# A hybrid decoder block: one spatial-gate product moves to head 6, one to the front of head 0, and the last row-sum turn goes behind an output product

## The chip, the cores and the metric

The kernel runs on one core of one Trainium2 chip. The metric is the device time of one execution in microseconds (us), lower is better. The core has TensorE (PE, with its weight loads shown as PEld), VectorE (DVE), ScalarE (ACT), GpSimd (POOL) and SyncE (SP, which issues nearly all DMAs here).

## The reference

The block takes x of 1024 tokens x 1024 channels in float32. Cut to what matters here:

```python
proj = rmsnorm(x, g1) @ w_in                 # q, k, v: 512 columns each; u, vg: 512 each; 8 forget gates
log_f = log_sigmoid(forget + b_forget)
att = forgetting_attention(q, k, v, log_f)   # 8 heads of 64; softmax(q k / 8 + c_i - c_j, causal) v
u, vg = split(gelu(uv))                      # 8 groups of 64 columns
sg = u * (tril(w_spatial) @ rmsnorm(vg) + b) # mixing inside chunks of 128 tokens
h = x + concat(att, sg) @ w_out              # 512 attention rows and 512 gate rows of w_out
h = h + conv_ffn(rmsnorm(h, g2), ...)        # up to 2 x 2816, causal conv of 3, silu gate, down
return rmsnorm(h, g_final)
```

## The kernel before

The work goes through stages: the projections, the spatial gate, attention, the output projection with the second norm, the up-projection with the convolution, and the down-projection. Matmul operands are split into a high part (rounded to fp32r) and the low rest, and each product is three matmuls: high x high, high x low, low x high. Except where the code fixes an order, the instructions of ScalarE, VectorE, GpSimd and SyncE are put in order at build time by a planner, which takes the earlier in the program among those whose inputs it expects to be ready. On TensorE the helper `seq` chains all instructions of the attention stage, so there the program's order holds.

**Attention.** The eight heads are cut into steps, `STEPS` (L1190), five for each head; step n is step `s = n % 5` of head `h = n // 5`, and holds two groups of attention blocks (the fifth holds one). The loop from L1226 does, in step n:

- `turn_p` (L1080) for the groups of step n+1: transposes of exponentials into a PSUM bank, a ScalarE cast to the high half (L1094) and a VectorE subtraction to the low half (L1095), both into a tile `pt`, of which there are three;
- `values` (L1100) for the groups of step n, on those halves (L1109), and where a half head is complete the evacuation to `attF` (L1117, L1118);
- for each group, the logits of one query block of the next head: four or fewer matmuls (L1021, L1022) into one of two buffers, and a VectorE pass (L1038) that adds the mask and takes the row minimum; the exponentials (L1062) come on ScalarE one step later;
- `fill` (L1194), which takes the next product of the spatial gate if `FILLS` (L22) names this step;
- copies of exponentials by DMA (`copy_p`, L1048), which make later transposes cheaper.

**Spatial-gate products.** `sg_out` (L1127) is a generator of 16 products, eight token blocks for each half of the output columns. Each is 12 matmuls (L1143 to L1145) of the transposed gate result `sgT` (four tiles, tag G) with split weights `whs` (four tiles, tag whl), a residual block loaded ahead (L1125), a VectorE add (L1147) and a store to `hpd` (L1148). At the seventh product the weights of the second half are loaded (`sg_load`); after the eighth, the list `SPLIT` has four splits, which the loop makes at L1295 to L1300, high half on ScalarE, low half on GpSimd. Three products stand before the loop (keys with head -1), the others in heads 0 to 5.

**Output projection, attention part.** `wo_load` (L1164) is called in step 35. It loads the four row blocks of `w_out` for attention and splits each on GpSimd (L1176, L1177), the first two into whl tiles and the other two into G tiles, four buffers of each tag. `pair_half` (L978) multiplies a pair of heads by its reciprocal row sums and splits it, on GpSimd (L984 to L986) for the first three pairs and on VectorE and ScalarE (L988 to L992) for the last; the third pair's result is a G tile too. `wmm` (L1180) makes output products (L1185); `EARLY` (L1188) puts those of the second and third weight block into steps 36 and 37.

**Row sums.** `row_tail` (L967) transposes the reciprocal row sums of a head (L972), copies them (L973), sends them to memory (L974, ScalarE's queue) and loads them back spread over 64 partitions (L975, SyncE's queue).

Of the kernel before, what the change touches and what calls it, by code (L numbers as in the profile page):

```python
# [18 lines left out]
NFF = 22  # L19
WARM = 8  # L20

FILLS = {(-1, j): 1 for j in (6, 4, 2)} | {(h, s): 1 for h in range(6) for s in ((0, 2, 4) if h == 0 else (2, 4))}  # L22
FCFG = ("b", 4, 4)


# [38 lines left out]
def after(tc, later, earlier):  # L64
    tc.add_manual_dep(later.ins, earlier.ins.name, mybir.DependencyInfo(
        mybir.DependencyClass.NoSync, mybir.DependencyReason.DATA), reason="order")
# [8 lines left out]
def block_kernel(ctx: ExitStack, tc: tile.TileContext, xT, xtok, wuv, wuh, wv0, wva, wvk, wvl, wqk, cpk, bfv,  # L75
# [10 lines left out]
    drm = ctx.enter_context(tc.tile_pool(name="drm", bufs=1, space=bass.MemoryType.DRAM))  # L86
    FILL = FILLS
    FTAG, FB, BB = FCFG
# [13 lines left out]
    def sb(tag, shape, dt=F32):  # L102
        return (base if tag == "x1" else raws if tag == "raw" else late if tag in LATE else early).tile(shape, dt, tag=tag, bufs=BUFS[tag], name=nm(tag))
# [10 lines left out]
    def f32(ap):  # L114
        return ap.bitcast(F32)
# [15 lines left out]
    for _ in range(WARM):  # L131
# [11 lines left out]
                       fill=MASK, base=0, channel_multiplier=1)  # L143
# [57 lines left out]
    def xs(n, hl, k):  # L201
        return XS[n][k // 2][hl][:, k % 2, :]
# [7 lines left out]
    def xr(n, k):  # L210
        return RAW[n][k // 2][:, k % 2, :]
# [89 lines left out]
    for o in (slice(0, 256), slice(256, 512)):  # L301
        h, l, src = xs("B11", 0, 0)[:, o], xs("B11", 1, 0)[:, o], xr("x11", 0)[:, o]
# [662 lines left out]
    exs, turns, due_copies, copied = [], {}, [], []  # L965
# [82 lines left out]
    def copy_p(h, i, ld=None):  # L1048

        w1, w2 = (2 * i + 1) * P, (2 * i + 2) * P  # L1050
        c = COLS[i] * P
        w1, w2 = w1 - c, w2 - c
        tp = sb(CTAG[i], [P, w1 + w2])
        turns[h, i] = (tp[:, 0:w1], tp[:, w1:w1 + w2])
        for jj in (1, 0):
            copied[:] = [sp.dma_start(out=turns[h, i][jj], in_=places[h, i][jj][:, c:])]
            if ld:
                after(tc, copied[0], ld)
# [62 lines left out]
    def residuals():  # L1121
        for hf in range(2):
            for tt in range(8):
                hs = sb("raw", [P, 512])
                yield hs, sp.dma_start(out=hs, in_=xtok[tt * P:(tt + 1) * P, hf * 512:hf * 512 + 512])  # L1125

    def sg_out(whs):  # L1127
        ready, source = [], residuals()
        for hf in range(2):
            o = slice(hf * 512, hf * 512 + 512)  # L1130
            for tt in range(8):
                ts_ = slice(tt * P, (tt + 1) * P)
                while len(ready) < (2 if due_copies else 1):
                    ready.append(next(source))
                while due_copies:
                    copy_p(*due_copies.pop(0), ready[-1][1])
                if hf == 0 and tt == 6:
                    nxt = sg_load(1, copied[0])
                hs = ready.pop(0)[0]
                ps = fbank()  # L1140
                for k in range(4):
                    w = whs[k]
                    seq(pe.matmul(ps, sgT[k][:, 0, ts_], w[:, 0, :], start=(k == 0), stop=False))  # L1143
                    seq(pe.matmul(ps, sgT[k][:, 0, ts_], w[:, 1, :], start=False, stop=False))  # L1144
                    seq(pe.matmul(ps, sgT[k][:, 1, ts_], w[:, 0, :], start=False, stop=(k == 3)))  # L1145
                def evac(ps=ps, hs=hs, tt=tt, o=o):
                    dve.tensor_tensor(out=hs, in0=ps, in1=hs, op=ALU.add)  # L1147
                    sp.dma_start(out=hpd[tt, :, o], in_=hs)  # L1148

                if dve.on:  # L1150
                    EVAC.append(evac)
                else:
                    evac()
                if hf == 0 and tt == 7:
                    whs = [None] * 4
                    SPLIT[:] = [(whs, k, nxt[k]) for k in range(4)]
                yield

    EVAC, SPLIT = [], []
# [20 lines left out]
    def wmm(tt, hf, ps, ks_):  # L1180
        ts_ = slice(tt * P, (tt + 1) * P)
        for k in ks_:
            w = wo[k][hf]
            for n, (a, b) in enumerate(((0, 0), (0, 1), (1, 0))):
                seq(pe.matmul(ps, attT[k][:, a, ts_], w[:, b, :], start=(k == 0 and n == 0), stop=(k == 3 and n == 2)))  # L1185

    banks8 = {}
    EARLY = {36: (1,), 37: (2,)}  # L1188
# [5 lines left out]
    def fill(key):  # L1194
        for _ in range(FILL.get(key, 0)):
            next(filler, None)
# [29 lines left out]
    for n, step in enumerate(STEPS):  # L1226
        h, s = n // 5, n % 5
        if s == 0 and h < 6:
            head_loads(h + 2)
        if h == 7 and s == 0:  # L1230
            for _ in filler:
                pass
            wo_load((0, 1))
            wo_load((2, 3))
        if h in (2, 4, 6) and s == 4:
            for o in (slice(0, 512), slice(512, 1024)):
                pair_half(h // 2 - 1, o)
        now, turned = turned, []
        last, due = due, []
        if n == 35:  # L1240
            psl.release()
            psl = tc.alloc_tile_pool(name="psc", bufs=4, space=bass.MemoryType.PSUM, reuse_waits="tile")
            banks8[0, 0] = lbank()
            wmm(0, 0, banks8[0, 0], (0,))
        for g in STEPS[n + 1] if n + 1 < len(STEPS) else []:
            if n == 36 and turned:
                for e in held + [mrow]:
                    after(tc, logits_exp(*e), casts[-1])
            turned.append(turn_p(g))
            if n == 36 and len(turned) == 2:  # L1250
                after(tc, casts[-1], exs[-1])
        if n == 34:
            mrow = (7, 0, logits_min(7, 0, mrow))
        if n == 33:

            held, last = last, []
        if n == 34:
            last, held = held[:1], held[1:] + last
        if n == 35:
            last, held = held[:1], held[1:]  # L1260
        if s == 1 and h % 2 == 0:
            attF[h // 2] = sb("H", [P, 2, 1024])
        if s == (1 if h < 7 else 2):
            recips[h] = dve.reciprocal(rows[h], rows[h])
        out_copy = None
        if n == 37:
            row_tail(7)
        if n in EARLY:
            wmm(0, 0, banks8[0, 0], EARLY[n])
        if n == 39:  # L1270
            banks8[4, 0] = lbank()
            wmm(4, 0, banks8[4, 0], (0,))
        for c, (g, pt, js) in enumerate(zip(step, now, NEXT[s])):
            out_copy = values(g, pt) or out_copy
            last_copy = out_copy
            if h < 7:
                for j in js:
                    if n == 33 and j == 0:
                        mrow = logits_mm(7, 0, place())
                        continue  # L1280
                    due.append((h + 1, j, logits_min(h + 1, j, logits_mm(h + 1, j, place()))))
            if s == 1 and h < 7 and c == 0:
                row_tail(h)

        for e in last:
            x = logits_exp(*e)
            after(tc, x, casts[-1] if n == 34 else out_copy or casts[-1])
        if s == 2 and h < 7:
            due_copies.extend(((h + 1, 3), (h + 1, 2)) if h < 6 else ((7, 3),))
        fill((h, s))  # L1290
        if s > 2 and h < 6:
            due_copies.append((h + 1, 4 - s))
        while due_copies:
            copy_p(*due_copies.pop(0))
        for _ in range(min(len(SPLIT), 1 if n == 9 else 2)):  # L1295
            ws_, k, wr = SPLIT.pop(0)
            wt = sb("whl", [P, 2, 512], F32R)
            ws_[k] = wt
            after(tc, act.copy(wt[:, 0], wr), out_copy or casts[-1])
            pool.tensor_tensor(out=wt[:, 1], in0=wr, in1=f32(wt[:, 0]), op=ALU.subtract)  # L1300
        if n == 2:
            vh = sb("A", [P, 2, 4, 256])
            sp.dma_start(out=vh, in_=vu.rearrange("h p m c -> p h m c"))
        if n in UPPER:
            tt = UPPER.index(n)
            v = V[tt // 2][:, tt % 2, 4:8]
            src = vh[:, tt // 4, tt % 4, :].rearrange("p (h d) -> p h d", h=4)
            after(tc, act.activation(src, src, AF.Copy, scale=rstd1[:, tt:tt + 1]), exs[-1])
            pool.tensor_copy(v[:, :, 0, :], src)
            pool.tensor_tensor(out=v[:, :, 1, :], in0=src, in1=f32(v[:, :, 0, :]), op=ALU.subtract)  # L1310
# [631 lines left out]
```

## Time and profile before

| what | us |
|---|---|
| median of 3 runs (1041.4 to 1042.5) | 1042.24 |
| the profiled execution, its time | 1042.4 |
| its span, first to last instruction | 1040.4 |
| TensorE busy | 1031.9 (99%) |
| VectorE busy | 890.5 (86%) |
| ScalarE busy | 563.7 (54%) |
| GpSimd busy | 242.2 (23%) |

In the profiled execution the projections and the gate end at about 207 us, the products before the loop at 223, the loop at 357, the output projection at 404, the up-projection at 825. Head 0 with its three products takes from 225.1 to 245.3; heads 1 to 5, with two each, some 17.7 each; from 333.8 the logits of head 7 have no product beside them.

Timeline rows give start, length, engine, line, operation and tiles, and in brackets the idle time of the engine before it with what ended it. Consecutive instructions of one kind are merged (x12), and a matmul's length overlaps with the next one's.

### The profile page before, as it was taken

The numbers are of one execution on the slowest core, as the hardware profiler recorded it, in microseconds if no ns is written. First come the engines' busy times: TensorE is split into PE (matmuls) and PEld (weight loads), VectorE is DVE, ScalarE is ACT, GpSimd is POOL, SyncE is SP. The second block draws the span as 40 slices with busy tenths as digits, with TensorE's granted clock in tenths as the row PEclk, the third lists the DMA queues.
The fourth block names the chain that finished last, engine by engine and source line by source line (L and its number), as shares of the span: only waits on it lengthen the run. The fifth ranks groups of instructions, "written<-read, shape, count | busy, mean of one in ns | idle before, by whom it ended". The sixth has DMA issues, their size and how long they took to land.

```text
span 1040.4 us, 14435 instructions
## 1 busy us (share of the span) xinstructions
PE 1031.9 (99%) x4998; PEld 865.6 (83%) x4998; DVE 890.5 (86%) x1294; ACT 563.7 (54%) x1004; POOL 242.2 (23%) x195
## 2 busy tenths in 40 slices
PE   9999999999999999999999999999999999999997
PEld 6988888988888888888888888888888888888886
DVE  6899887888888888998999998998997866997774
ACT  6777533457876757654444443444544554444654
POOL 0000242512733640433334323333331000000000
PEclk9999999999999999999999999999999999999999
DMA  9622558897978652231354432432322998333432
GB/s 336 221 97 83 163 150 247 232 252 224 275 249 258 231 165 99 82 122 62 136 178 139 132 115 72 132 101 86 116 82 93 324 332 294 110 92 101 149 117 99
DMA packets 73708, 170.25 MB, mean 164 GB/s; under 512 B 8718, under 2 KB 12934, under 8 KB 73636
## 3 DMA queue, kind: packets, MB, share of 16 engines
q1 hardware_dynamic: 73364, 169.30, 50.8%
q8 instruction: 39, 0.64, 0.2%
q14 instruction: 33, 0.27, 0.1%
q10 hardware_dynamic: 272, 0.04, 0.0%
HBM read 112.53 MB, written 45.05 MB: 151 GB/s over the span
## 4 chain that ended last, share of the span: by engine, by line
PE 94%; DVE 2%; ACT 2%; DMA 1%; issue 1%; SPq 0%; ACTq 0%; DVEq 0%
PE pb L1488 23%; PE pk L1488 17%; PE pb L1752 11%; PE pk L1752 9%; PE ps L286 4%; PE pk L1185 4%; PE pb L1109 3%; PE pb L286 3%; PE qc L525 2%; PE qd L525 2%; PE qa L525 2%; PE ps L876 2%; PE pl L1021 1%; PE pl L1022 1%; PE pf L1143 1%; PE pf L1144 1%
## 5 line engine op out<-in xcount | busy, mean ns | idle before, releaser
L1488 PE MATMUL pb<-xT,whb 128*128 128x512 f32 x804 | 189.4, 389 | 0.0
L1488 PEld LDWEIGHTS pb<-xT,whb 128*128 128x128 f32 x804 | 150.8, 188 | 31.4
L1488 PE MATMUL pk<-xB,x 128*128 128x512 f32 x528 | 127.2, 390 | 0.0
L1752 PE MATMUL pb<-whb,x 128*128 128x512 f32 (+1 forms) x528 | 119.2, 387 | 0.0
L1488 PEld LDWEIGHTS pk<-xB,x 128*128 128x128 f32 x528 | 98.8, 188 | 20.8 <-DVE x L175 0.4
L1752 PEld LDWEIGHTS pb<-whb,x 128*128 128x128 f32 x528 | 98.3, 188 | 20.3 <-DVE x L175 0.2
L169 ACT CAST x<-sg 128x512 fp32r<-128x512 f32 x77 | 47.8, 622 | 96.6 <-PE pk L1752 45.7
L169 ACT CAST whb<-sg 128x512 fp32r<-128x512 f32 x82 | 50.4, 617 | 83.9 <-PE pb L1488 82.1
L1752 PE MATMUL pk<-whb,x 128*128 128x512 f32 (+1 forms) x408 | 91.8, 386 | 0.0
L1752 PEld LDWEIGHTS pk<-whb,x 128*128 128x128 f32 x408 | 75.9, 188 | 15.5
L175 DVE TENSOR_TENSOR x<-sg,x 128x512 fp32r<-128x512 f32 x77 | 52.8, 688 | 39.4 <-ACT x L169 39.2
L1538 DVE SCALAR_TENSOR_TENSOR ca<-h,cp,ca 128x1023 f32<-128x1023 f32 (+1 forms) x44 | 68.3, 1552 | 3.7 <-ACT ca L1537 3.6
L1538 DVE SCALAR_TENSOR_TENSOR cg<-h,cp,cg 128x1023 f32<-128x1023 f32 (+1 forms) x44 | 65.5, 1489 | 5.2 <-ACT cg L1537 4.9
L1488 PE MATMUL pb<-xB,whb 128*128 128x512 f32 x264 | 63.9, 389 | 0.0
L175 DVE TENSOR_TENSOR whb<-sg,whb 128x512 fp32r<-128x512 f32 x82 | 57.4, 701 | 4.7 <-ACT whb L169 4.6
L1488 PE MATMUL pk<-xT,whb 128*128 128x512 f32 x252 | 61.0, 389 | 0.0
L1385 POOL TENSOR_TENSOR sg<-raw 128x512 f32<-128x512 f32 x20 | 29.5, 1475 | 132.1 <-DVE whb L175 73.0
L1094 ACT CAST pt<-pb 128x512 fp32r<-128x512 f32 x72 | 40.2, 583 | 34.5 <-PE pb L1090 20.9
L1488 PEld LDWEIGHTS pb<-xB,whb 128*128 128x128 f32 x264 | 49.5, 188 | 10.7 <-issue 0.4
L1095 DVE TENSOR_TENSOR pt<-pb,pt 128x512 fp32r<-128x512 f32 x72 | 47.5, 687 | 11.5 <-ACT pt L1094 10.8
L1488 PEld LDWEIGHTS pk<-xT,whb 128*128 128x128 f32 x252 | 47.2, 188 | 10.0 <-DVE whb L175 0.3
L1109 PE MATMUL pb<-pt,V 128*128 128x512 f32 (+3 forms) x192 | 48.8, 359 | 0.1
(425 smaller groups left out, 2167.1 us busy)
## 6 DMA issues: line engine op xcount, KB each, us to landing
raw<-wup SPq DMA_DIRECT2D x44, 512.0 KB
sg<-hx SPq DMA_DIRECT2D x77, 256.0 KB
hx<-hs SPq DMA_DIRECT2D x44, 256.0 KB
hx<-ca SPq DMA_DIRECT2D x35, 256.0 KB
xT<-wdn SPq DMA_DIRECT2D x28, 256.0 KB
x<-kd SPq DMA_DIRECT2D x18, 256.0 KB
A<-xtok SPq DMA_DIRECT2D x8, 512.0 KB
raw<-wqk SPq DMA_DIRECT2D x8, 512.0 KB
```

The costliest lines, as they stand in the source:

```text
L169: cast[:] = [act.copy(h, src)]
L175: return eng.tensor_tensor(out=l, in0=src, in1=f32(h), op=ALU.subtract)
L286: pe.matmul(banks[m], xs(n, xi, k)[:, ms], w[:, wi, :], start=(first and k == 0 and c == 0 and (own or m % 2 == 0)), stop=(k == 3 and c == ...
L525: pe.matmul(ps, w[:, wi, ks], xs(n, xi, k), start=(first and c == 0), stop=(c == 11), skip_group_check=True)
L1094: casts.append(act.copy(pt[:, 0, :], ptr))
L1095: los.append(dve.tensor_tensor(out=pt[:, 1, :], in0=ptr, in1=f32(pt[:, 0, :]), op=ALU.subtract))
L1109: seq(pe.matmul(po[half][:, o:o + w], lhs, pt[:, s, c:c + w], start=(new and s == 0), stop=(s == 1 and (half, k) in ((1, 6), (0, 3))), ski ...
L1185: seq(pe.matmul(ps, attT[k][:, a, ts_], w[:, b, :], start=(k == 0 and n == 0), stop=(k == 3 and n == 2)))
L1385: pool.tensor_tensor(out=s[0], in0=a21, in1=a22, op=ALU.add)
L1488: pe.matmul(ps, w[:, wi, ks], xb[:, xi, k, :], start=(first and n == 0), stop=(n == 11), skip_group_check=True)
L1538: return [dve.scalar_tensor_tensor(out=c[:, n:1024], in0=h[:, 0:1024 - n], scalar=w[2 - n], in1=c[:, n:1024], op0=ALU.mult, op1=ALU.add) f ...
L1752: pe.matmul((banks[bk + m] if ps is None else ps)[:, o], xh[:, xi, ms], wh[:, wi, o], start=((first and p_ == 0 or new) and n == 0), stop= ...
```

## The change

Three things. The product of key (0, 4), at the end of head 0's last step, is dropped from `FILLS`, and (6, 2), the end of head 6's third step, is added, so that all products from the sixth on move to the next place in the list; where no residual is left to load ahead, the generator now takes None. The product of key (0, 0) is taken at the front of step 0, before the turns for step 1, instead of at its end. In step 37 the early output product stands before `row_tail(7)` instead of behind it. The special case for step 9, in which one split was made instead of two, goes.

```diff
-FILLS = {(-1, j): 1 for j in (6, 4, 2)} | {(h, s): 1 for h in range(6) for s in ((0, 2, 4) if h == 0 else (2, 4))}
+FILLS = {(-1, j): 1 for j in (6, 4, 2)} | {(h, s): 1 for h in range(6) for s in ((0, 2) if h == 0 else (2, 4))} | {(6, 2): 1}
...
                 while len(ready) < (2 if due_copies else 1):
-                    ready.append(next(source))
+                    ready.append(next(source, None))
                 while due_copies:
-                    copy_p(*due_copies.pop(0), ready[-1][1])
+                    copy_p(*due_copies.pop(0), (ready[-1] or ready[-2])[1])
...
         now, turned = turned, []
         last, due = due, []
+        if n == 0:
+            fill((0, 0))
...
         out_copy = None
+        if n in EARLY:
+            wmm(0, 0, banks8[0, 0], EARLY[n])
         if n == 37:
             row_tail(7)
-        if n in EARLY:
-            wmm(0, 0, banks8[0, 0], EARLY[n])
...
-        fill((h, s))
+        if n:
+            fill((h, s))
...
-        for _ in range(min(len(SPLIT), 1 if n == 9 else 2)):
+        for _ in range(min(len(SPLIT), 2)):
```

## The prediction

> **What bounds the kernel now.** I read the page first (the chain of waits), then the table by stage, then TensorE's timeline through the attention stage, and beside it those of VectorE, GpSimd and SyncE at each place that the edit touches.
>
> ```profile
> span 1040.4 us, 14435 instructions
> ...
> PE 94%; DVE 2%; ACT 2%; DMA 1%; issue 1%; SPq 0%; ACTq 0%; DVEq 0%
> ```
>
> ```profile
> 357.00:404.00 47.00, 47.00 (x236) 39.39 (x236) 40.09 (x59) 26.91 (x52) 12.70 (x8) 1.00 0.54 183
> ```
>
> TensorE carries 94% of the chain, and behind the attention stage it runs without a break: the second fence is one stretch of the table (length, then busy time of PE, PEld, DVE, ACT, POOL, granted clock, DMA share, GB/s), 47.00 of 47.00 us. The edit leaves the number of matmuls as it is, so it can only fill TensorE's gaps or open new ones, and a microsecond won or lost up to 357 us is one at the end. A matmul that waits for its second operand already counts as busy; I therefore read gaps from the distances of starts.
>
> **Front of head 0.** A product group is 12 matmuls, one residual add on VectorE, and a load and a store of 256 KB on SyncE's queue. The sixteen transposes at 223.04 are the turns of groups 0 to 3; the values of group 0 follow.
>
> ```profile
> 207.05 1.91 PE L846 MATMUL ps<-ident,A 128*128 128x128 f32 x16
> 208.80 1.91 PE L846 MATMUL pb<-ident,A 128*128 128x128 f32 x16
> ...
> 223.04 1.93 PE L1093 MATMUL pb<-ident,C 128*128 128x128 f32 x16
> 225.12 0.73 PE L1109 MATMUL pb<-pt,V 128*128 128x512 f32 x2
> ```
>
> ```profile
> 224.38 0.69 DVE L1095 TENSOR_TENSOR pt<-pb,pt 128x512 fp32r<-128x512 f32 x1
> ```
>
> Sixteen such transposes cost 1.75 us at 207.05 and 2.08 here: TensorE waits 0.33 for VectorE's low half of group 0, which ends at 225.07. The edit puts a product between the turns of groups 0, 1 and those of groups 2, 3, so the wait is covered: **-0.33**. VectorE gets the add at about 226.9, where it would wait for the later turns anyway, and the minima of head 1 after it; by the second product of head 0 it has room again. If that cover is missing the gain is 0, which is the other bound.
>
> **Head 0's last step.** Here a product leaves.
>
> ```profile
> 242.49 0.45 PE L1143 MATMUL pf<-whl,G 128*128 128x512 f32 x1
> ...
> 245.27 0.80 PE L1090 MATMUL pb<-ident,C 128*128 128x128 f32 x8
> 245.91 0.71 PE L1109 MATMUL pb<-pt,V 128*128 128x512 f32 x2
> ```
>
> ```profile
> 253.82 0.38 PE L1021 MATMUL pl<-x,x 128*128 128x384 f32 x1
> ```
>
> ```profile
> 243.08 1.29 DVE L1095 TENSOR_TENSOR pt<-pb,pt 128x512 fp32r<-128x512 f32 x2 [0.45 <-ACT pt L1094]
> ...
> 245.07 0.20 DVE L1264 RECIPROCAL rs<-rs 128x8 f32<-128x8 f32 x1
> 245.47 0.69 DVE L1147 TENSOR_TENSOR raw<-pf,raw 128x512 f32<-128x512 f32 x1 [0.20 <-PE pf L1145]
> 246.48 1.49 DVE L1095 TENSOR_TENSOR pt<-pb,pt 128x512 fp32r<-128x512 f32 x2 [0.31 <-ACT pt L1094]
> ...
> 253.33 0.08 DVE L1038 DVE_READ_ACCUMULATOR2_ANT mn<- 128x1 f32 x1
> ```
>
> TensorE's work from 245.27 on would stand 2.78 us earlier (245.27 - 242.49). The values of group 0 of head 1 would start at 243.13, but their low half is VectorE's work from 243.08 to 243.7, and the second matmul asks for it at 243.36: 0.4 of stall at once. Behind it VectorE works almost without rest, 243.08 to 245.27 and then (the residual add at 245.47 drops out) 246.48 to 253.41, together 9.1 us; the minimum that ends at 253.41 would end at 252.2. The last logits before the next product, 253.82 today, need the buffer that it frees and would stand at 251.04: late by 1.15. About 0.2 of the 9.1 are short waits that shrink. I take **+0.9**; bounds 0.4 (the first stall alone) and 1.3. The next product lets VectorE catch up, so no more is late behind it.
>
> **The later second half.** All products from the sixth on shift by one place, and with them the loads of the second half's weights (SyncE, behind one more step's copies, with two steps to land) and their splits, from steps 9 to 11 to steps 12 and 13. The first product on them opens at the last step of head 2 instead of its third.
>
> ```profile
> 273.90 0.39 PE L1143 MATMUL pf<-whl,G 128*128 128x512 f32 x1
> 274.32 0.50 PE L1144 MATMUL pf<-whl,G 128*128 128x512 f32 x1
> 274.66 0.39 PE L1145 MATMUL pf<-whl,G 128*128 128x512 f32 x1
> ```
>
> ```profile
> 272.97 1.30 POOL L1300 TENSOR_TENSOR whl<-raw,whl 128x512 fp32r<-128x512 f32 x1
> ```
>
> Today the last split (GpSimd, to 274.27) holds that product up by 0.3 us (steps of 0.42 and 0.34 instead of 0.23). Afterwards the last two splits, 1.3 each and one behind the other, fall into the step just before the product. If ScalarE casts for them early the 0.3 is won; if it does so behind that step's exponentials, I estimate them 0.7 too late, 0.4 worse than now. I take **0**, the middle; bounds -0.3 and +0.4.
>
> **Head 6.** The moved product stands behind the logits of step 32, at 342.67.
>
> ```profile
> 328.09 0.71 PE L1109 MATMUL pb<-pt,V 128*128 128x256 f32 x4
> 328.63 0.28 PE L1021 MATMUL pl<-x,x 128*128 128x256 f32 x1
> ```
>
> ```profile
> 342.67 0.22 PE L1090 MATMUL pb<-ident,gg 128*128 128x128 f32 x1
> ...
> 342.97 0.70 PE L1109 MATMUL pb<-pt,V 128*128 128x256 f32 x4
> 343.92 0.38 PE L1021 MATMUL pl<-x,x 128*128 128x256 f32 x1 [0.25 <-DVE mn L1038]
> ...
> 351.98 0.38 PE L1093 MATMUL pb<-ident,wy 128*128 128x128 f32 x2
> 352.50 0.27 PE L972 MATMUL pb<-ident,rs 128*8 128x128 f32 x1
> 352.53 0.94 PE L1185 MATMUL pk<-G,G 128*128 128x512 f32 x3
> ```
>
> Head 5, which has a product there, goes from values to logits in 0.54 us; here it takes 0.95, a stall of 0.41 that a cover of 2.7 us removes. The row-sum turn at 352.50 starts 0.52 after the last two transposes, which take 0.22: 0.30 of waiting, hidden once the output product goes first. Together **-0.71**; 0 if something else ends last there.
>
> Something does. The four split weights and the four transposed gate tiles are now read until this product. Their buffers (tags whl and G, four each) are what GpSimd next writes the third head pair (lines 984 to 986) and the output weights (1176, 1177) into.
>
> ```profile
> 333.57 0.61 POOL L985 CAST G<-H 128x512 fp32r<-128x512 f32 x1
> 334.12 0.62 POOL L1176 CAST whl<-raw 128x512 fp32r<-128x512 f32 x1
> ...
> 335.95 1.29 POOL L984 TENSOR_TENSOR H<-H 128x512 f32<-128x512 f32 x1
> ...
> 346.78 2.57 POOL L1177 TENSOR_TENSOR G<-raw,G 128x512 fp32r<-128x512 f32 x2
> ...
> 363.35 1.67 POOL L1378 TENSOR_TENSOR raw<-raw,raw 128x512 f32<-128x512 f32 x1 [10.40 <-DVE G L992]
> ```
>
> From 334.12 to the first low half of the third weight (346.78 + half of 2.57 = 348.06) GpSimd works 13.9 us on end. Changed, one multiplication (1.3) is done before the wait and one more cast (333.57 to 334.12, 0.55) falls behind it: 13.2. It can't start before the product's third matmul has ended, 342.67 + 2 x 0.23 + 0.40 = 343.5; the low half is there at 356.7. TensorE asks for it in the second matmul of the early output product of the third weight: 342.67 + 2.74 (twelve matmuls) + 9.53 (342.67 to 352.20) - 0.41 + 0.23 = 354.8. **+1.9**, in three waits, since the first and second weights are late as well. Bounds: 0, if the order on GpSimd serves each early product in time, and 3.2, with the multiplication in the row again.
>
> Queued behind this wait are, on TensorE, the row-sum turn (now second) and, through it, the last row sums; on GpSimd nothing until 363.35, behind 10.40 of idle time; on SyncE the up-projection loads that reuse the raw blocks.
>
> The Trainium skill ("PSUM — Partial Sum Buffer", Engine vs sequencer instructions) has matmuls start and complete in program order. By it the waiting output product holds the row-sum turn too, until about 357; by an engine that passes waiting matmuls, the turn would leave near 355, and the sum would be the same while the row sums have margin. The trace agrees: at 352.50 the output product, whose weight was ready since 348.06, stood behind the waiting turn.
>
> **Sum.** -0.33 + 0.9 + 0 - 0.71 + 1.9 = +1.8 us. The profiled execution took 1042.4, its span of 1040.4 and 2.0 around it, 0.16 above the median of 1042.24. On the median: **1044.0 us**. A measurement of this kernel tells about 0.2%, 2.1 us, from no change; this is a loss just inside it.
>
> **Rivals.** (1) *Not slower: GpSimd isn't late.* Without the 1.9: -0.1, **1042.1**; with head 0 at its lower bound and the splits early, -0.9, **1041.3**. For it: GpSimd's order today is interleaved, not the program's, so it may put first what TensorE needs first. Against: the first two weights (four halves of 0.55 and 1.3 each) stand ahead of the third in today's row.
>
> (2) *Clearly slower: the last row sums end last.*
>
> ```profile
> 355.17 0.47 SPq L975 DMA_DIRECT2D H<-rsd  x1
> ```
>
> ```profile
> 361.97 1.29 DVE L992 TENSOR_TENSOR G<-H,G 128x512 fp32r<-128x512 f32 x2 [1.03 <-ACT G L991]
> ```
>
> ```profile
> 364.50 2.88 PE L1185 MATMUL pk<-G,G 128*128 128x512 f32 x12
> ```
>
> Their chain runs from the turn (352.50) over the load on SyncE (355.17) to the last low half at 363.3, and TensorE wants that at 365.2 (three matmuls into the row at 364.50): 1.9 of margin, 1.2 once the turn stands behind an output product of 0.7. The turn leaves at 357.2, its load at 359.9. If SyncE keeps ahead of it a load that waits for GpSimd's last weight (356.7 + 1.25 + 3.7 = 361.7), it leaves 1.8 late or more, and 512 KB before it take 2.9 at 183 GB/s. The rival decides from 1.2 late; with one such load in front it costs 3.5: **1047.5**. Against: this load waits for nothing of GpSimd.
>
> (3) *Losses and gains cancel*, **1042.3**: the waits it aims at sum to 1.0 us (0.33 + 0.71), and VectorE's lag may come out at its lower bound while ScalarE and GpSimd are reordered.
>
> **Chances.** Forecast 0.45 (same 0.25, slower 0.20, since 1044.3 is the mark), rival 1 0.30 (same 0.23, faster 0.07), rival 2 0.15 (slower), rival 3 0.10 (same 0.08, faster 0.02): faster 0.09, same 0.56, slower 0.35. The range goes from below rival 1's second value, 1040.8, to 1046.2, which leaves most of rival 2 out.
>
> **What would show it.** Right: the values of group 0 follow their turns without a gap; head 1's first values wait 0.4 us on VectorE; GpSimd idles from about 335 until 0.9 us into the last product and then works 18 us on end; lines 1185 of the last head wait for line 1177, two microseconds in all; the logits of step 33 don't wait. Wrong: the early output products run without a wait on GpSimd, head 1 opens without a stall, or the row of output products behind 364 waits for the row sums.

## The result and the profile after

The changed kernel takes **1052.99 us** (median; 1051.95 to 1054.63), the kernel before, measured beside it, 1042.08 (1041.40 to 1044.89). The ratio is 1.0103, with a 95% interval of 1.0088 to 1.0118: 1% slower, clear of noise, and 6.8 us over the upper end of the predicted range. The profiled execution of the changed kernel took 1052.05, so it is one of the faster of the six; its span is 1050.2, 9.8 longer than that of before. Below the diff's places all line numbers are 3 higher than before (1374 is 1377, 1406 is 1409); lines 972 to 1185 keep theirs.

The span and the chain of waits, from the page:

```profile
span 1050.2 us, 14437 instructions
...
PE 94%; POOL 2%; DMA 2%; ACT 1%; DVE 1%; issue 0%; SPq 0%; DVEq 0%; POOLq 0%; ACTq 0%
```

GpSimd isn't in the list of before; now it has 2% of the chain. The stretch of the table that was without a break has one (length, then busy time of PE, PEld, DVE, ACT, POOL, granted clock, DMA share, GB/s):

```profile
357.00:404.00 47.00, 42.82 (x208) 35.24 (x206) 33.95 (x50) 23.18 (x44) 16.51 (x13) 0.96 0.60 184
```

TensorE is idle for 4.2 of the 47 us, and its clock is 0.96 on average instead of 1.00. Where that comes from stands in five timelines. **TensorE, head 0's end:**

```profile
241.57 0.50 PE L1090 MATMUL pb<-ident,C 128*128 128x128 f32 x4
242.90 0.53 PE L1090 MATMUL pb<-ident,C 128*128 128x128 f32 x4 [0.82 <-DVE pt L1095]
243.50 0.72 PE L1109 MATMUL pb<-pt,V 128*128 128x512 f32 x2
...
246.89 0.69 PE L1109 MATMUL pb<-pt,V 128*128 128x512 f32 x2
247.75 0.50 PE L1021 MATMUL pl<-x,x 128*128 128x512 f32 x1 [0.17 <-DVE mn L1038]
...
250.34 0.71 PE L1109 MATMUL pb<-pt,V 128*128 128x512 f32 x2
251.08 0.50 PE L1021 MATMUL pl<-x,x 128*128 128x512 f32 x1
```

Eight such transposes take 0.64 before (245.27 to 245.91); four of them take 1.33 here, then 0.60: 1.0 and 0.3 of waiting for VectorE's low halves. Twice more the logits come late, 0.86 and 0.74 after the start of the values instead of 0.55, the first time held by VectorE's pass, and each time their second matmul follows 0.1 later than usual. Together 2.0.

**GpSimd, then TensorE, at the end of attention:**

```profile
332.75 1.29 POOL L984 TENSOR_TENSOR H<-H 128x512 f32<-128x512 f32 x1 [1.90 <-DVE H L1118]
342.75 1.17 POOL L985 CAST G<-H 128x512 fp32r<-128x512 f32 x2 [8.71 <-PE pf L1145]
...
354.71 2.51 POOL L1177 TENSOR_TENSOR G<-raw,G 128x512 fp32r<-128x512 f32 x2
357.18 1.16 POOL L1176 CAST G<-raw 128x512 fp32r<-128x512 f32 x2
358.31 2.53 POOL L1177 TENSOR_TENSOR G<-raw,G 128x512 fp32r<-128x512 f32 x2
```

```profile
347.62 0.44 PE L1185 MATMUL pk<-whl,A 128*128 128x512 f32 x1
348.83 0.73 PE L1185 MATMUL pk<-whl,A 128*128 128x512 f32 x2 [0.77 <-POOL whl L1177]
...
351.79 0.47 PE L1185 MATMUL pk<-whl,A 128*128 128x512 f32 x1
352.44 0.73 PE L1185 MATMUL pk<-whl,A 128*128 128x512 f32 x2 [0.18 <-POOL whl L1177]
...
354.65 0.48 PE L1185 MATMUL pk<-G,G 128*128 128x512 f32 x1
356.03 0.73 PE L1185 MATMUL pk<-G,G 128*128 128x512 f32 x2 [0.91 <-POOL G L1177]
356.60 0.27 PE L972 MATMUL pb<-ident,rs 128*8 128x128 f32 x1
```

GpSimd idles 8.71 until the moved product has freed its buffers, then works from 342.75 to 360.84 on end. Each early output product waits for it at its second matmul: steps of 1.21, 0.65 and 1.38 instead of 0.23, together 2.6. The row-sum turn leaves right behind the last of them, at 356.60.

**SyncE's queue, first of before with GpSimd's last split there, then of the changed kernel** (start, time from the first issue of the group to the end of the last):

```profile
349.37 3.93 SPq L1374 DMA_DIRECT2D raw<-wup  x2
```

```profile
350.38 2.57 POOL L1177 TENSOR_TENSOR G<-raw,G 128x512 fp32r<-128x512 f32 x2
```

```profile
357.25 3.94 SPq L1377 DMA_DIRECT2D raw<-wup  x2
361.30 0.80 SPq L1409 DMA_DIRECT2D pt<-hpd  x1
362.15 0.47 SPq L975 DMA_DIRECT2D H<-rsd  x1
```

Loads of this size take 0.3 to 1.2 us each to issue elsewhere in this queue (0.80 in the second row). Each of these two takes 0.33, but from the first to the end of the second pass 3.9 us: the second one waits for the raw block that GpSimd's last split reads, and leaves at 360.87. Before, that split ended at 352.95 (the row at 350.38), and the row-sum load behind it left at 355.17, 2.7 after its turn. Now the split ends at 360.84, the block is freed, the load goes, then a load of partial sums, and only then the row sums, at 362.15, 5.5 after their turn and 7 us later than before. (The chain view gives the landing of the first load, at the same moment, as what released the second. In rowload_first, below, the second leaves only 1.1 us after the first, at 361.39, again 0.03 after the end of GpSimd's last split, so it is the split.)

**The end of that chain**, VectorE and then TensorE, and the table by stage (columns as above):

```profile
370.35 1.29 DVE L988 TENSOR_TENSOR H<-H 128x512 f32<-128x512 f32 x2 [7.01 <-DMA H<-rsd]
```

```profile
367.42 0.84 PE L1185 MATMUL pb<-G,G 128*128 128x512 f32 x3
372.44 4.79 PE L1185 MATMUL pk<-G,G 128*128 128x512 f32 x12 [4.18 <-ACT G L991]
377.06 0.85 PE L1185 MATMUL pb<-G,G 128*128 128x512 f32 x3
```

```profile
372.00:374.00 2.00, 1.56 (x5) 1.04 (x6) 2.00 (x4) 0.29 (x1) 0.90 (x1) 0.81 0.37 148
374.00:376.00 2.00, 2.00 (x6) 1.62 (x5) 2.00 (x3) 0.00 (x0) 1.92 (x2) 0.50 0.00 0
376.00:378.00 2.00, 2.00 (x9) 1.54 (x9) 1.84 (x4) 1.43 (x4) 2.00 (x3) 0.84 0.35 139
```

The row sums arrive 8.2 us after their issue (362.15 to 370.35). TensorE waits for them 4.3 us (372.44 less 367.42, less 0.68 for three matmuls), and then works at half its clock for 3.4 us (373.2 to 376.6): the twelve matmuls take 4.62 (to 377.06) where they took 2.72.

The 9.8 us by stretches of TensorE's timeline. Up to the moved product: it starts at 341.75, where before the same place stood at 342.67 with one product (2.73) more ahead of it: +1.8. From there to the last row: 30.7, of which 2.7 are the product, before 21.8: +6.1. The row itself: +1.9.

### The profile page after: what moved, and what is told of

It reads as the page before. It is cut to its first block, busy times and chain, and to the rows that moved or that the text cites. A ratio compares the mean times of both kernels' runs of the same rounds, so it can differ in the third digit from the quotient of the medians.

```text
span 1050.2 us, 14437 instructions
## 1 busy us (share of the span) xinstructions
PE 1035.4 (99%) x4998; PEld 866.2 (82%) x4998; DVE 888.7 (85%) x1294; ACT 565.0 (54%) x1004; POOL 242.3 (23%) x195
## 4 chain that ended last, share of the span: by engine, by line
PE 94%; POOL 2%; DMA 2%; ACT 1%; DVE 1%; issue 0%; SPq 0%; DVEq 0%; POOLq 0%; ACTq 0%
PE pb L1491 23%; PE pk L1491 17%; PE pb L1755 11%; PE pk L1755 9%; PE ps L286 5%; PE pb L286 5%; PE pk L1185 3%; PE pb L1109 2%; PE qc L525 2%; PE qd L525 2%; PE qa L525 2%; PE ps L876 2%; PE pl L1021 2%; PE pl L1022 1%; PE pf L1144 1%; PE pf L1145 1%
## 5 line engine op out<-in xcount | busy, mean ns | idle before, releaser
L1095 DVE TENSOR_TENSOR pt<-pb,pt 128x512 fp32r<-128x512 f32 x72 | 47.6, 688 | 14.2 <-ACT pt L1094 13.4
```

The lines of the kernel that those rows point to most:

```text
L1095: los.append(dve.tensor_tensor(out=pt[:, 1, :], in0=ptr, in1=f32(pt[:, 0, :]), op=ALU.subtract))
```

## The experiments

Each ran beside the kernel before, on the same chip; its medians were 1041.85 to 1041.99 there. Where a kernel has a line more ahead of a place, line numbers are higher by one to six.

**rowload_first: the order on SyncE's queue.**

```diff
-        sp.dma_start(out=wr, in_=wup[i, :, 0:2, :])
+        after(tc, sp.dma_start(out=wr, in_=wup[i, :, 0:2, :]), rowld[7])
```

`rowld[7]` is the load of line 975 for head 7.

> The changed kernel, with one order added on SyncE: both up-projection loads of line 1377 come behind the load of the last row sums (line 975 of head 7). Theory A (the order on SyncE's queue): the load leaves about 359.5 instead of 362.15, no block waits for GpSimd ahead of it, the 4.3 us gap at the last row of output products goes and with it the 1.9 us of lowered clock: 1053.0 - 6.2 = 1046.8 us; GpSimd's idle stretch and the three waits of 2.5 us stay. Rival B (GpSimd's late weights and the turn held behind them make the row sums late, whatever the queue's order): the last row of output products still waits 3 us or more, 1051 to 1053 us.

Measured: 1046.81 us (1046.03 to 1047.13), ratio 1.0044 [1.0030, 1.0058]. SyncE's queue, VectorE and TensorE:

```profile
359.73 0.47 SPq L976 DMA_DIRECT2D H<-rsd  x1
360.30 1.43 SPq L1378 DMA_DIRECT2D raw<-wup  x2
```

```profile
364.51 1.29 DVE L989 TENSOR_TENSOR H<-H 128x512 f32<-128x512 f32 x2 [0.68 <-DVE x L175]
```

```profile
368.58 2.88 PE L1186 MATMUL pk<-G,G 128*128 128x512 f32 x12
```

The load leaves at 359.73, 2.6 us after its turn, as before the change, and VectorE starts 4.8 us after that. Its 0.68 of idle time may still be for this load, since the line that the bracket names ended at 363.83; TensorE doesn't feel it. The last row has no bracket and takes its 2.7 us; the clock is 1.00 in each stretch from 360 to 384. One order on one queue takes away 6.2 us, while GpSimd's idle time and the three waits on it are as in the changed kernel. Theory A holds, rival B falls. The order does two things at once: the load leaves 2.9 us sooner after its turn (2.6 instead of 5.5), and its sums are in use at least 3.4 us sooner after it has left (4.8 instead of 8.2), with other loads around it. Which of those loads make the second part isn't shown.

**turn_back: the third part of the change undone.**

```diff
+        if n == 37:
+            row_tail(7)
         if n in EARLY:
             wmm(0, 0, banks8[0, 0], EARLY[n])
-        if n == 37:
-            row_tail(7)
```

> The changed kernel with its third part undone: the last row-sum turn stands ahead of the output product again. SyncE's order then is: both up-projection loads, the row-sum load, the first partial-sum load (in the changed kernel the last two are the other way round). Theory A: the row-sum load still stands behind the up-projection load that waits for GpSimd and leaves at 361.3, with 512 KB less in front of it (2.9 us at 183 GB/s): the gap is 1.4 us instead of 4.3; with 0.3 for the turn's own wait 1053.0 - 2.9 + 0.3 = 1050.4 us if the clock falls all the same, 1048.5 us if so short a gap leaves it alone. Rival B (what makes the row sums late is that TensorE holds the turn behind the waiting output product): the turn leaves 3 us earlier, no gap, 1047.1 us.

Measured: 1049.90 us (1049.26 to 1051.62), 1.0077 [1.0064, 1.0091].

```profile
358.62 3.94 SPq L1377 DMA_DIRECT2D raw<-wup  x2
362.65 1.01 SPq L975 DMA_DIRECT2D H<-rsd  x1
```

```profile
372.05 4.62 PE L1185 MATMUL pk<-G,G 128*128 128x512 f32 x12 [2.79 <-ACT G L991]
```

The row-sum load still leaves right after the blocked loads, although its turn stands earlier: the place of the turn on TensorE isn't the cause. With one load less in front the gap is 2.8 to 3.0 us; I had expected 1.4, with 2.9 us for the load left out, and it saved about 1. The clock falls all the same in the profiled execution, so the 1050.4 of the expectation fits in time, with another split. But that execution is the slowest of the four (1051.62; the others 1049.26 to 1049.98), and whether the clock fell in the others isn't shown.

**move_only: the moved product alone.**

```diff
-FILLS = ... ((0, 2, 4) if h == 0 else (2, 4))}
+FILLS = ... ((0, 2) if h == 0 else (2, 4))} | {(6, 2): 1}
```

(against the kernel before; the None for a missing residual and the end of the special case for step 9 come with it.)

> The kernel before with one part of the change alone: the product moves from head 0's last step to head 6; none at the front of head 0, the row-sum turn where it was. Theory A: it brings head 0's stall (1.8), the splits (0.3), GpSimd's waits (2.5) and the row-sum load behind the blocked up-projection load with the short gap (1.4), less 0.41 at step 33: 1042.1 + 5.6 = 1047.7 us, or 1049.6 us with a lowered clock; nearly all of the loss comes with this part. Rival B (the turn's place is needed for the loss): only 1042.1 + 4.2 = 1046.3 us and no wait for the last row sums.

Measured: 1050.78 us (1049.55 to 1054.89), 1.0090 [1.0073, 1.0108].

```profile
370.14 3.21 PE L1185 MATMUL pk<-G,G 128*128 128x512 f32 x12 [1.77 <-ACT G L991]
...
377.92 1.06 PE L1438 MATMUL pb<-ident,xn 128*128 128x128 f32 x8 [1.17 <-DVE ss L1419]
```

This part alone makes 8.8 of the 10.9 us, the wait for the row sums with it; rival B's 1046.3 is out, and theory A's upper figure, 1049.6, is 1.2 too low. In the profiled run, the fastest of the four, the gap is 1.8 us, the clock stays at 1.00 and the row takes 3.05 us; but then the turns of the first normed row (line 1438) wait 1.3 us for VectorE, which is late by the same row sums (they arrive at 368.05, and the chain view goes from there over VectorE's rows to these turns). What the clock doesn't take, that wait takes in part.

**front_turn: the two other parts.**

```diff
-FILLS = ... ((0, 2) if h == 0 else (2, 4))} | {(6, 2): 1}
+FILLS = ... ((0, 2, 4) if h == 0 else (2, 4))}
```

(against the changed kernel; one split in step 9, as before.)

> The kernel before with the two other parts: head 0's first product goes to its front, and the row-sum turn stands behind the output product; head 0 keeps its last product, head 6 gets none. Theory A: 0.33 and 0.30 us are won, GpSimd isn't late; on SyncE the first partial-sum load now stands ahead of the row-sum load, 512 KB more, which the margin of 1.2 to 1.9 us may not cover: 1041.5 us if it does, up to 1043.2 us if not. Rival B: with the turn behind the output product the row sums are late here too, and the time is over 1045 us.

Measured: 1041.62 us (1041.15 to 1042.74, 11 runs) beside 1041.99; 0.9997 [0.9988, 1.0006]. The span is 1039.7, 0.7 shorter than that of before, and both waits are gone from TensorE's timeline. The row-sum load leaves at 355.05, 2.6 us after its turn, though the turn stands behind the output product and a partial-sum load ahead of the load: neither makes the row sums late by itself, and rival B falls. As for time, a gain of 0.6 can't be told from nothing by these runs. It is the best version found, and not shown to beat the kernel before.

**halves_alone and halves: GpSimd's order.**

```diff
+            seq_ = ((0, 0), (0, 1), (1, 0), (2, 0), (1, 1), (2, 1))
+            for a, b in zip(seq_, seq_[1:]):
+                after(tc, wlo[b][0], wlo[a][1])
```

The pairs are weight block and half; `wlo` holds the cast and the low half of each. `halves_alone` is the changed kernel with this, `halves` is rowload_first with this.

> The changed kernel with that order on GpSimd alone; SyncE's queue as in the changed kernel. GpSimd's last weight is ready no earlier, so the blocked up-projection load and the row-sum load behind it leave no earlier. Theory A (the last row sums end last, so GpSimd's waits ahead of them cost nothing in the changed kernel): the waits shrink by 2.1 us and the gap at the last row grows by as much, 6.4 us: 1053.0 us. Rival D (the losses add up): 1050.9 us.

Measured: 1053.09 us (1051.92 to 1055.05), 1.0113 [1.0098, 1.0129].

```profile
354.43 0.94 PE L1190 MATMUL pk<-G,G 128*128 128x512 f32 x3
...
372.55 4.74 PE L1190 MATMUL pk<-G,G 128*128 128x512 f32 x12 [5.72 <-ACT G L991]
```

The third early product runs without a wait (its three matmuls in one row), and the gap at the last row grows from 4.2 to 5.7 us of idle time; the row starts at 372.55, against 372.44. The waits shrink by 1.35, not by the 2.1 of the expectation. In the changed kernel GpSimd's waits ahead of the last row cost nothing of their own: a chain that runs past TensorE sets its end.

> The kernel of rowload_first (row-sum load ahead of the up-projection loads) with one more order, on GpSimd: the halves of the output weights are split one by one, and the first half of the third weight ahead of the second half of the second. The first low half comes 0.55 us earlier and the first half of the third weight 1.9 earlier. Theory A (GpSimd's row is what TensorE waits for in the three places): of the 2.5 us the first wait keeps 0.4 and the other two go: 1046.8 - 2.1 = 1044.7 us. Rival C (those waits are TensorE's own or come from the loads of the weights): 1046.8 us.

Measured: 1047.57 us (1046.84 to 1048.47), 1.0055 [1.0041, 1.0069]: a miss, no gain over 1046.81.

```profile
352.97 0.74 PE L1191 MATMUL pk<-whl,A 128*128 128x512 f32 x2 [0.42 <-POOL whl L1178]
355.21 0.94 PE L1191 MATMUL pk<-G,G 128*128 128x512 f32 x3
...
374.57 1.06 PE L1447 MATMUL pb<-ident,xn 128*128 128x128 f32 x8 [0.84 <-DVE ss L1428]
```

The first wait shrinks from 1.0 to 0.5 and the third goes, but the second grows from 0.4 to 0.7, since TensorE comes to it earlier: 1.35 less in all. The last row then starts at 367.45 instead of 368.58, and 1.0 is given back at the turns of the first normed row, which wait for VectorE: it starts the last pair at 364.70, no sooner than in rowload_first (364.51), though the row-sum load left 1.1 us sooner, at 358.60. So GpSimd's order does set the three waits, rival C's reason falls, but the gain doesn't reach the end.

**to_head5 and from_head5: head 0 and GpSimd apart.**

```diff
-... | {(6, 2): 1}
+... | {(5, 3): 1}
```

> The changed kernel with the moved product at step 3 of head 5 instead of step 2 of head 6: the last product stands where it stood before, so GpSimd's buffers come free as before; head 0 loses its last product, front and row-sum turn as changed. Theory A: what is left is head 0's stall (1.8 us) and the splits (0.4), less 0.31 at the front and 0.30 at the row-sum turn: 1042.0 + 1.6 = 1043.6 us; no wait on GpSimd, none for the last row sums. Rival E (head 0's stall is only moved time, caught up by the next products): 1041.5 us.

Measured: 1044.30 us (1043.65 to 1046.18, 8 runs), 1.0027 [1.0017, 1.0037]. The stall of 1.0 at head 0's last step is there as in the changed kernel, no early product waits for GpSimd, the last row has no gap:

```profile
243.38 0.53 PE L1090 MATMUL pb<-ident,C 128*128 128x128 f32 x4 [0.82 <-DVE pt L1095]
```

Head 0's loss is a real one, and rival E falls. The time is 0.7 over theory A's 1043.6. The span is 2.1 longer than that of before: head 0's stall and the splits make 2.5 of loss, more than the 2.2 of the expectation, and the two small gains take 0.7 back, which leaves 0.3 unexplained.

```diff
-FILLS = ... ((0, 2) if h == 0 else (2, 4))} | {(6, 2): 1}
+FILLS = ... ((0, 2, 4) if h == 0 else (2,) if h == 5 else (2, 4))} | {(6, 2): 1}
```

(with the order of rowload_first)

> Front and row-sum turn as changed, the row-sum load ahead of the up-projection loads as in rowload_first, head 0 keeps its last product; the product that goes to step 2 of head 6 is taken from head 5's last step instead. Theory A (a product that late costs GpSimd's buffers, whatever place it comes from): the three waits on GpSimd, 2.5 us, are here without head 0's stall; less 0.31, 0.30 and 0.41 (step 33); head 5's last step loses its cover, from 0 (no stall there) to 1.8 us (as in head 0): 1042.0 + 1.5 = 1043.5 to 1045.3 us. Rival H (GpSimd is late only because the splits of the second half came later): no wait on GpSimd, 1041.0 us plus what head 5 loses.

Measured: 1045.70 us (1044.25 to 1046.43), 1.0034 [1.0020, 1.0048].

```profile
331.22 0.54 PE L1091 MATMUL pb<-ident,C 128*128 128x128 f32 x4 [0.72 <-DVE pt L1096]
...
354.90 0.73 PE L1186 MATMUL pk<-G,G 128*128 128x512 f32 x2 [0.90 <-POOL G L1178]
```

The stall that head 0's end showed is now at head 5's end: it belongs to a last step without a product. The wait on GpSimd is there although the splits stand where they stood: rival H falls. The time is 0.4 over the upper end; here too, the turns of the first normed row wait 1.1 us for VectorE.

**keep_busy and keep_busy8: the clock.**

```diff
+            if (tt, hf) == (0, 0):
+                wb = bank()
+                for _ in range(16):
+                    seq(pe.matmul(wb, attT[2][:, 0, 0:P], wo[2][0][:, 0, :], start=True, stop=True))
             wmm(tt, hf, ps, (3,) if (tt, hf) in early_ else range(4))
```

> The changed kernel with 16 extra matmuls (3.6 us, their result read by nobody) ahead of the last row of output products, where TensorE has its 4.3 us gap. Theory F (the lowered clock comes from the gap): the clock stays at 1.00 and the row's matmuls take 0.23 instead of 0.43 us, 1.85 us won, of which the next turns, which wait for VectorE (1.3 us in the kernel with the move alone), may take back 1.3: 1051.2 to 1052.5 us. Rival G (the row's matmuls are slow for another reason, such as the transfers then under way): they stay at 0.43 us, 1053.0 us.

Measured: 1052.33 us (1050.47 to 1053.30), 1.0098 [1.0084, 1.0112].

```profile
368.35 3.79 PE L1477 MATMUL pb<-G,G 128*128 128x512 f32 x16
372.78 3.21 PE L1185 MATMUL pk<-G,G 128*128 128x512 f32 x12 [0.64 <-ACT G L991]
...
380.57 1.06 PE L1441 MATMUL pb<-ident,xn 128*128 128x128 f32 x8 [1.18 <-DVE ss L1422]
```

With TensorE kept busy the row takes 3.05 us instead of 4.62: the lowered clock comes from the gap, and rival G falls. It is worth little: of the 1.6 us, 1.3 come back as a wait for VectorE at the normed row, and the median, 0.7 lower, lies inside the spread of the changed kernel's runs.

> As keep_busy, with 8 extra matmuls (1.8 us) instead of 16, so that some 2.5 us of the gap stay. The gap of 2.95 us in turn_back brought the clock to 0.50, that of 1.94 us in the kernel with the move alone did not. If the length of the gap alone decides, the clock falls here when the bound is under 2.5 us (matmuls of 0.43 us, as in turn_back) and stays when it is over 2.5; either way the bound is narrowed to a half.

Measured: 1052.17 us (one run).

```profile
372.77 4.38 PE L1185 MATMUL pk<-G,G 128*128 128x512 f32 x12 [2.74 <-ACT G L991]
```

The row sums came a little later than in keep_busy, and 2.74 us of the gap were left, not 2.5: the clock fell. So this run bounds the clock's limit no tighter than turn_back.

## Why the prediction was wrong

The forecast was +1.8 us, the result is +10.9. Step by step:

- **Front of head 0, -0.33: right.** The values follow their turns without a gap (the turns at 226.21, the values 0.79 later, as eight transposes take); from the loop's start to the first row-sum turn it is 0.4 less.
- **Head 0's last step, +0.9 with bounds 0.4 to 1.3: mechanism right, size too small.** It measured 2.0. I let the first stall come at the values, 0.4. But the second group's turns stand ahead of them, and the row at 242.90 shows these waiting for VectorE's low half, 1.0, probably for the PSUM bank that it frees (argued from the code, not tried alone); I had asked only who reads the low half. to_head5 confirms the loss.
- **The later second half, 0 (-0.3 to +0.4): just over the upper end.** The product takes 3.63 us (276.11 to 279.74), 0.80 more than the one in the same place of the next head, with steps of 0.67 and 0.40; before, the one that waited took 3.05, 0.28 more than the one in its place a head later. That is 0.5 more, the case of a late ScalarE cast.
- **Head 6 and the row-sum turn, -0.71: right.** The logits of step 33 follow the values without a wait, the turn its output product.
- **GpSimd late, +1.9: right in place and order, a little small.** GpSimd starts one microsecond into the product, goes through the predicted 18 us row, and the three waits sum to 2.6. The third weight's first low half is there 14.2 after the product's start (forecast 14.0); without its waits TensorE would have asked for it 11.7 after (forecast 12.1). The prediction's remark that a waiting matmul counts as busy holds only for short waits: of the 0.98 before 348.83 the profile shows 0.77 as idle.
- **"Against: this load waits for nothing of GpSimd": the step that failed.** It is true of the row-sum load's own data and buffer. But the loads in SyncE's queue leave in order, and the load two places ahead waits for GpSimd's last weight: the row sums left 5.5 us after their turn, not 2.7, and the last row waited 4.3 for them. Setting them ahead of it (rowload_first) took 6.2 us away. I had worked out when that weight is done, 361.7 (it was 360.84), and what the load behind it would cost, and then gave that rival 0.15. The row of before that points to it was in SyncE's timeline: two up-projection loads at 349.37 that take 3.93 us to issue, until GpSimd's last split ends at 352.95. It stood ahead of the row-sum load before, with 2 us of margin, and GpSimd's last split came 7.9 later. I read the queue by what its loads need, not by how long each stood at its head.
- **The price of that rival, 3.5, was too small as well.** There were two loads of 512 KB in the way (a partial-sum load had come ahead too, since the turn stands later), the row sums took 8.2 us to arrive, and the gap was 4.3. turn_back, without the second of them, has 3.0 and 7.3 us to arrive: that load cost about 1, not the 2.9 at which I priced it. With one load of 512 KB ahead that was not held (rowload_first) it is 4.8, so the rate in the table, 183 GB/s, doesn't give the delay.
- **Nothing in the sum allowed for the clock.** The row at 372.44 took 1.9 us longer than before, 1.6 of it by the clock (keep_busy has the same row in 3.05). The Trainium skill ("TensorE: Matmul & The Clock Gate", HAM oscillation) warns of idle gaps over about 3.4 us, and the trace agrees with its gap of 4.2, though 2.8 was enough in turn_back. That a wait of this size costs more than its own length belongs to the price of a rival that opens one.

The sum with the measured terms: -0.4 (front) + 2.0 (head 0) + 0.5 (splits) - 0.7 (head 6 and turn) + 2.6 (GpSimd) + 4.3 (row sums) + 1.9 (the row itself, mostly clock) = 10.2, for 9.8 of span; this execution also came to the products before the loop 0.5 earlier (211.84 against 212.34), at a place that the edit doesn't touch. These are a chain's terms and don't stand alone: halves_alone takes 1.35 away from GpSimd's term and wins nothing, as the last row then waits about as much longer. The medians are 10.9 apart and the profiled executions 9.65: the changed kernel's runs spread from 1051.95 to 1054.63, and what makes the slower of them slower isn't shown.

The row sums aren't the whole miss. The five terms that the forecast did have make 4.0 as measured, not 1.8: all but the front and head 6 came out larger. rowload_first, where the row sums cost nothing, is still 4.8 us slower than the kernel before (4.2 of span); its 1046.81 is 0.6 over the upper end of the predicted range.

The Trainium skill's rule in the prediction ("PSUM — Partial Sum Buffer", Engine vs sequencer instructions), that matmuls start in program order, is borne out: the turn at 356.60 left behind the product that had waited until 356.03, with its own operand there since 353.62. It was the right rule for the smaller part of the delay.

## What to carry to other kernels

Read an in-order DMA queue by its issue rows: a group of loads that takes microseconds to leave, where one issue takes 0.33 us, holds a wait, and all that stands behind it has the margin of that wait, not its own. When a change makes one engine late, look for each buffer that this engine frees, for the load that waits for the buffer, and for what is queued behind that load. Where several waits lie on one engine ahead of a chain that runs past it, taking away the earlier ones only lengthens the last: find the chain that ends last first.

## What the runs showed of the hardware

In the profiled executions the granted clock fell to 0.50 with idle times of TensorE of 2.74 (keep_busy8), 2.79 (turn_back), 4.18 (changed kernel) and 5.72 us (halves_alone), and stayed at 1.00 with 1.77 (move_only) and 0.64 (keep_busy). The lowered clock lasted 3.4 us in three of the four (373.2 to 376.6 in the changed kernel), and twice that, 6.8, in halves_alone (369.5 to 376.3). It didn't begin at a fixed point of the gap: in keep_busy8 2.3 us after TensorE went idle, in turn_back 1.4 us after TensorE had started again.

The page of the Trainium skill named above gives about 3.4 us as the window. The lowered stretches have that length, but less idle time was enough. A bound between 1.8 and 2.7 fits these six runs; since the fall comes at such different points of a gap, where a window happens to begin may have its part, which they can't tell.

A load of 256 KB was in use 8.2 us after its issue with two loads of 512 KB issued up to 1.3 us ahead of it and three more within 1.6 us behind it (changed kernel), 7.3 us with one of the two ahead (turn_back), and 4.8 us with one load of 512 KB 0.4 us ahead of it and two within 1.7 us behind it (rowload_first).
